# First block's boundaries reordered and the second softmax of the differential heads left in PSUM

## The chip, the cores and the metric

The kernel runs on one core of one Trainium2 chip. A core has a matrix engine (PE, TensorE) and three engines for element work: DVE (VectorE), ACT (ScalarE) and POOL (GpSimd). Each works through its own instructions in program order and waits on semaphores for the others. SP issues the DMA transfers of the weights. Matrix products land in PSUM, eight banks of 128 partitions x 512 fp32; everything else is in SBUF. The metric is the device time of one execution in microseconds; the kernel before takes 1145.21 us (median of 3 runs, 1144.27 to 1145.81).

## The reference

Two transformer stacks run one behind the other on one sequence of 256 tokens, width 1024, fp32. The first is one block with three sublayers: feed-forward, a mixer of two attentions, feed-forward.

```python
mods = (silu(c) @ w_ada + b_ada).reshape(B, 9, 1024)   # shift, scale, gate of 3 sublayers
n = modulate(rmsnorm(h, g_pre[0]), shift(0), scale(0))
h = h + 0.5 * gate(0) * rmsnorm(swiglu(n, ...), g_post[0])
n = modulate(rmsnorm(h, g_pre[1]), shift(1), scale(1))
p = n @ w_in            # qa, ka, va, qi, ki, wi, qb, kb, vb
# oa: each query keeps the top 64 keys of an index score sum_h relu(qi_h . ki) * wi_h, then softmax
# ob: stick-breaking attention
h = h + gate(1) * rmsnorm(concat(oa, ob) @ w_out, g_post[1])
n = modulate(rmsnorm(h, g_pre[2]), shift(2), scale(2))
h = h + 0.5 * gate(2) * rmsnorm(swiglu(n, ...), g_post[2])
```

The second has two layers. The first of them begins with differential attention, 8 heads of two softmaxes each; the other has latent attention, and both have a squared-ReLU network.

```python
q, k, v = split(rms_norm(h, g) @ w_qkv)       # q, k rotated; (B, S, 8 heads, 2, 64), v (B, S, 8, 128)
p = softmax(where(causal, q @ k.T * 64 ** -0.5, -inf))
a = p[:, :, 0] - lam * p[:, :, 1]             # the two softmaxes of a head, combined
o = rms_norm(a @ v, subln_g, 1e-5) * (1 - lambda_init)
h = h + o @ w_o
```

## The kernel before

**Precision and tiles.** A product is three passes: each weight tile of 128 x 1024 is split into `wh` (ACT, L475) and `wl`, raw minus `wh` (DVE or POOL by `st["lo"]`, L481), and each activation likewise into `nh` and `nl`; the PE multiplies `wh` by `nh`, `wh` by `nl` and `wl` by `nh` (`mm`, L534). So nothing can be multiplied until both halves of its activation are there.

**Weights.** They come in one fixed order in pieces of up to 512 KB over SP's queue into a ring of seven `raw` tiles. `pump` takes the next piece from the ring and issues its split, as far ahead of the PE as `st["ahead"]` lets it. Pieces of the modulation matrix (`ada`) are mixed in: for one of them ACT first writes eight copies into an accumulator (L445), and DVE adds the piece to it (L448). As the engines work in order, a piece that is pumped stands in front of everything that is issued after it on ACT and on DVE or POOL.

**PSUM.** Four banks belong to accumulators (`abank`); the other four (`bank`, tile name `mm`) are a ring for transposes, scores and small products.

**Entry into a sublayer of the first block.** `enter_block1` ends one sublayer and begins the next for two row blocks of 128 tokens. `tail` is the rest of the old product; `Post` normalizes and adds it (`sq`: square sum, L594; `u_`: product with the gain, L658; `b`: inverse root; `c`: the sum into h, L669). `Pre1` normalizes h for the new sublayer (`stat`, `r_`, `yy`: L688), transposes it in eight tiles of 128 (`T`, L619), modulates each tile by its column's scale and shift (`mod`, DVE L642 or ACT L640), and splits the result into `nh` (ACT, L709) and `nl` (DVE, L712). p0 and q0 stand for row block 0, p1 and q1 for row block 1. `direct` modulates on ACT straight into `nh`, while DVE modulates the same tiles again into a PSUM bank (`y2_`), from which the low half is formed. `mid[0]` and `mid[1]` are the first products of the new sublayer that are put between. The function runs twice: into the mixers (the first entry, up to about 235 us), where `mid` is `kiva`, the product for the index keys, the index weights and part of the values, and into the second feed-forward network (the second entry, 365 to 395 us), where `mid` is `f2.mul` of `Ffn2` and `f2.act` is silu (L927) and its product with the other half (L928).

**Index keys.** `keys()` (L1223) normalizes the index keys, copies the values, and has the keys transposed (L1240) and written back by ACT (L1241, `kiT`). The scores, their sum over heads (DVE, L1263) and the search for the top 64 (DVE, `topk`) follow; in that search POOL makes the low halves of the weights.

**Differential heads.** For each pair of heads `qk_finish` rotates queries and keys (DVE L1476, L1478, POOL L1480) and transposes them. `head` multiplies them into two banks, one for each softmax, and `softmax_bank` takes each to its exponentials: DVE adds the mask and finds the extremum (L1487) into the SBUF tile `s`, and ACT takes the exponential in place (L1490). Then DVE combines the two (L1572, `SCALAR_TENSOR_TENSOR`, two pieces of 256 and 128 columns), the PE transposes the result (L619) and multiplies it with v.

## Time and profile before

| | |
|---|---|
| median of 3 runs | 1145.21 us (1144.27 to 1145.81) |
| the profiled execution | 1145.55 us, of it the span 1143.7 us |
| PE busy | 1102.1 us (96% of the span) |
| DVE busy | 745.5 us (65%) |
| ACT busy | 610.0 us (53%) |
| POOL busy | 147.2 us (13%) |
| mean granted clock of the PE | 0.991 |

The span is the time from the first to the last instruction that the profiler recorded. A share of busy time is a mean over stages: an engine busy for 65% of the span can be full for 30 us in one of them. The granted clock is a share of the PE's full 2.4 GHz; 0.5 is its lower level, 1.2 GHz. A row of the timeline has a start, a duration (several like instructions in one row have a common duration) and, in brackets, the idle time before it with the instruction that ended it. `nl<-mm,nh` means that tile `nl` is written from `mm` and `nh`; buffer numbers are left out.

### The profile page before, as it was taken

To read this page: it belongs to the slowest core of one execution; us is meant where nothing else is said; L and a number is where in the kernel's file an instruction comes from. 1 tells how busy PE (TensorE), PEld (TensorE's weight loads), DVE (VectorE), ACT (ScalarE), POOL (GpSimd) and SP (SyncE) were. 2 spreads that over 40 slices of the span, in tenths; PEclk is the share of its full clock that TensorE was granted. 3 is DMA by queue.
4 is the path that set the end of the run, shared out by engine and by line. 5 is a ranking of instruction groups with operands and counts; after the bars stand their busy time and mean duration, and the time that the engine had idled before them with its cause. 6 is when DMAs were issued, how large, how long until landed. Compare 5 with 4: busy or idle time off the path is not lost. (4 is left out here: it accounts for less than half of the span.)

```text
span 1143.7 us, 18702 instructions
## 1 busy us (share of the span) xinstructions
PE 1102.1 (96%) x7156; PEld 994.6 (87%) x7156; DVE 745.5 (65%) x1306; ACT 610.0 (53%) x1181; POOL 147.2 (13%) x203
## 2 busy tenths in 40 slices
PE   6999999999999899999999899999999999999997
PEld 5998999888887799999877779999999888999996
DVE  6978777789686865554655457555566766655554
ACT  5564445654676643443564666444457665544442
POOL 1002000214002000000069840000002200000001
PEclk8999999999999999999999999999999999999999
DMA  9979897377565485555444245555544533655541
GB/s 324 403 244 352 332 335 229 121 251 294 168 208 198 166 313 189 180 186 185 164 148 147 99 161 175 193 185 186 189 159 138 194 111 138 248 187 188 191 136 38
DMA packets 65915, 230.26 MB, mean 201 GB/s; under 512 B 7272, under 2 KB 8688, under 8 KB 65696
## 3 DMA queue, kind: packets, MB, share of 16 engines
q1 hardware_dynamic: 63792, 225.06, 56.4%
q10 hardware_dynamic: 1776, 3.29, 0.8%
q8 instruction: 56, 0.92, 0.3%
q0 software_dynamic: 256, 0.71, 0.3%
q14 instruction: 35, 0.29, 0.1%
HBM read 227.97 MB, written 2.63 MB: 202 GB/s over the span
## 5 line engine op out<-in xcount | busy, mean ns | idle before, releaser
L481 DVE TENSOR_TENSOR wl<-raw,wh 128x1024 fp32r<-128x1024 f32 (+3 forms) x319 | 381.6, 1212 | 75.1 <-ACT wh L475 74.9
L475 ACT ACTIVATE wh<-raw 128x1024 fp32r<-128x1024 f32 (+3 forms) x350 | 355.3, 1035 | 29.2 <-DMA raw<-in_stream_dram 26.1
L534 PE MATMUL mm<-nl,wh 128*128 128x256 f32 x1128 | 314.3, 283 | 0.0
L534 PE MATMUL mm<-nh,wh 128*128 128x256 f32 x1128 | 314.1, 283 | 0.0
L534 PE MATMUL mm<-nh,wl 128*128 128x256 f32 x1128 | 314.1, 283 | 0.0
L534 PEld LDWEIGHTS mm<-nh,wh 128*128 128x128 f32 x1128 | 214.2, 192 | 3.1
L534 PEld LDWEIGHTS mm<-nl,wh 128*128 128x128 f32 x1128 | 214.2, 192 | 3.0
L534 PEld LDWEIGHTS mm<-nh,wl 128*128 128x128 f32 x1128 | 213.8, 192 | 0.1
L534 PE MATMUL acc<-wh,fh 128*128 128x512 f32 x372 | 120.8, 392 | 0.0
L534 PE MATMUL acc<-wh,fl 128*128 128x512 f32 x372 | 119.8, 389 | 0.3 <-DVE fl L904 0.3
L534 PE MATMUL acc<-wl,fh 128*128 128x512 f32 x372 | 119.8, 389 | 0.0
L481 POOL TENSOR_TENSOR wl<-raw,wh 128x256 fp32r<-128x256 f32 (+2 forms) x124 | 91.0, 773 | 197.8 <-ACT wh L475 197.8
L1086 ACT ACTIVATE rl<-mm 128x256 f32<-128x256 f32 x64 | 24.6, 384 | 159.0 <-PE mm L534 159.0
L591 POOL TENSOR_TENSOR sm<-sm,nhalf 128x1 f32<-128x1 f32 (+1 forms) x36 | 22.4, 624 | 629.1 <-DVE sm L600 561.2
L1087 DVE TENSOR_TENSOR ff<-rl 128x256 f32<-128x256 f32 x64 | 27.2, 425 | 101.8 <-ACT rl L1086 101.8
L899 ACT ACTIVATE sg<-mm 128x256 f32<-128x256 f32 x38 | 14.5, 382 | 139.2 <-PE mm L534 139.2
L534 PEld LDWEIGHTS acc<-wh,fl 128*128 128x128 f32 x372 | 69.9, 188 | 15.7 <-DVE fl L904 0.9
L534 PEld LDWEIGHTS acc<-wl,fh 128*128 128x128 f32 x372 | 69.9, 188 | 15.0
L534 PE MATMUL acc<-wh,nh 128*128 128x512 f32 (+3 forms) x216 | 80.4, 395 | 0.5 <-ACT nh L709 0.4
L534 PE MATMUL acc<-wh,nl 128*128 128x512 f32 (+3 forms) x216 | 77.2, 380 | 3.6 <-DVE nl L712 3.6
L534 PE MATMUL acc<-wl,nh 128*128 128x512 f32 (+3 forms) x216 | 76.6, 377 | 0.0
L534 PEld LDWEIGHTS acc<-wh,fh 128*128 128x128 f32 x372 | 65.5, 189 | 9.1
(316 smaller groups left out, 1591.8 us busy)
## 6 DMA issues: line engine op xcount, KB each, us to landing
raw<-in_stream_dram SPq DMA_DIRECT2D x395, 512.0 KB, 4.6
raw<-in_stream_dram SPq DMA_DIRECT2D x16, 448.0 KB, 8.9
raw<-in_stream_dram SPq DMA_DIRECT2D x8, 384.0 KB, 3.7
raw<-in_stream_dram SPq DMA_DIRECT2D x8, 292.0 KB, 2.9
gp<-in_rows_dram SPq DMA_DIRECT2D x3, 512.0 KB, 6.6
wide<-scr ACTq DMA_DIRECT2D x1, 1536.0 KB, 9.9
raw<-in_stream_dram SPq DMA_DIRECT2D x4, 320.0 KB, 2.7
h<-in_x_dram SPq DMA_DIRECT2D x4, 256.0 KB, 3.5
```

What stands on the lines that cost most here:

```text
L475: act.activation(wh[:, 0:n], raw, AF.Copy)
L481: e.tensor_tensor(wl[:, u:v], raw[:, u:v], wh[:, u:v].bitcast(F32), op=ALU.subtract)
L534: pe.matmul(o, l, r, start=start, stop=True, skip_group_check=True)
L591: pool.tensor_tensor(o, v, nhalf[:, 0:v.shape[-1]], op=ALU.pow)
L899: act.activation(sg, ps[:, 0:S], AF.Silu)
L1086: act.activation(rl, ps[:, 0:S], AF.Relu)
L1087: dve.tensor_tensor(ff, rl, rl, op=ALU.mult)
```

## The change

There are four edits.

1. **POOL's pieces.** Where POOL makes a low half of more than 512 columns, it does so in two pieces and not in four.
2. **The boundary code.** `direct` is gone: every modulated tile is written once, and both halves are formed from it. In row block 0 the first four tiles are modulated by DVE into two PSUM banks, two tiles in each; the last four are modulated by ACT into SBUF. In row block 1 DVE's four and ACT's four all go into SBUF. High and low halves are formed in pairs of tiles. `p1.u_(0)` stands behind the first low halves of row block 0. `mid[0]` is issued ahead of the pumped weights, and a new argument, `aside`, is issued ahead of the transposes of row block 1; the second entry gives it `f2.act(0)`, which stood behind the whole entry.
3. **The index keys.** The constant `G5` (8) is written out; its loops keep their order. The last of eight `pump` calls in the loop over k moves behind `begin(keys())`.
4. **The heads.** `softmax_bank` can write its exponentials to another place than it reads. For the second softmax of each head that place is the PSUM bank which held its scores, and the combine reads it there.

```diff
@@ -50,7 +50,6 @@
 EL1 = ((1, 2), 1)
 EL2 = ((0, 1), 0)
 G4 = 7
-G5A = 8
 GSP = {2: 1, 8: 1}
 LO0 = "pool"
 YH = (1, 1, 1, 1, 1)
@@ -475,10 +474,10 @@
         act.activation(wh[:, 0:n], raw, AF.Copy)
         c = n * {"dve": 8, "alt": 4, "pool": 0}.get(st["lo"], st["lo"]) // 8
         for e, a, b in ((dve, 0, c), (pool, c, n)):
-            step = b - a if e is dve or b <= a else (b - a) // (4 if b - a > 512 else 2)
-            for u in range(a, b, step or 1):
-                v = min(u + step, b)
-                e.tensor_tensor(wl[:, u:v], raw[:, u:v], wh[:, u:v].bitcast(F32), op=ALU.subtract)
+            m = (a + b + 1) // 2 if b - a > 512 and e is pool else b
+            for u, v in ((a, m), (m, b)) if b > a else ():
+                if v > u:
+                    e.tensor_tensor(wl[:, u:v], raw[:, u:v], wh[:, u:v].bitcast(F32), op=ALU.subtract)
         st["w"] += 1
         tiles[key] = (wh, wl)
 
@@ -672,7 +671,7 @@
     class Pre1:
         def __init__(self, i, n, t):
             self.i, self.n, self.t, self.ss = i, n, t, small(2)
-            self.y, self.tp = [None, None], [None, None]
+            self.y, self.tp, self.y2 = [None, None], [None, None], {}
 
         def stat(self, hf):
             square_sum(half(self.t, hf), D, self.ss[:, hf:hf + 1])
@@ -691,28 +690,21 @@
             self.tp[hf] = transposes(self.y[hf], 4)
 
 
-        def y2_(self, a, b, on_act=False):
-            if a == 0:
-                self.y2 = [bank() for _ in range(2)]
+        def y2_(self, a, b, on_act=False, psum=False):
+            y = (bank() if psum else w512("y2"))[:, 0:(b - a) * P].rearrange("p (a b) -> p a b", b=P)
             for k in range(a, b):
-                c = slice(k % 4 * P, k % 4 * P + P)
-                mod(self.i, k, self.y2[k // 4][:, c], self.tp[k // 4][:, c], on_act)
-
-        def direct(self, a, b):
-            for k in range(a, b):
-                mod(self.i, k, self.n[0][:, k, tk(self.t)], self.tp[k // 4][:, k % 4 * P:k % 4 * P + P], True)
-
-        def y2v(self, a, b):
-            return self.y2[a // 4].rearrange("p (a b) -> p a b", a=4)[:, a % 4:a % 4 + b - a, :]
-
-        def hi(self, a, b):
-            act.activation(self.n[0][:, a:b, tk(self.t)], self.y2v(a, b), AF.Copy)
-
-        def lo(self, a, b):
-            dve.tensor_tensor(self.n[1][:, a:b, tk(self.t)], self.y2v(a, b),
-                              self.n[0][:, a:b, tk(self.t)].bitcast(F32), op=ALU.subtract)
-
-    def enter_block1(tail, acc, G, i, n, mid, table, early, late):
+                mod(self.i, k, y[:, k - a, :], self.tp[k // 4][:, k % 4 * P:k % 4 * P + P], on_act)
+                if k % 2 == 0:
+                    self.y2[k] = y[:, k - a:k - a + 2, :]
+
+        def hi(self, k):
+            act.activation(self.n[0][:, k:k + 2, tk(self.t)], self.y2[k], AF.Copy)
+
+        def lo(self, k):
+            dve.tensor_tensor(self.n[1][:, k:k + 2, tk(self.t)], self.y2[k],
+                              self.n[0][:, k:k + 2, tk(self.t)].bitcast(F32), op=ALU.subtract)
+
+    def enter_block1(tail, acc, G, i, n, mid, table, early, late, aside=None):
 
         p0, p1 = Post(acc, G, 0), Post(acc, G, 1)
         q0, q1 = Pre1(i, n, 0), Pre1(i, n, 1)
@@ -737,38 +729,49 @@
             pump_n(k)
         tail.go(1, 0, m)
         p1.sq(0)
-        p1.u_(0)
         q0.T(0)
         q0.T(1)
         tail.go(1, 1, m)
-        q0.direct(0, 2)
-        q0.y2_(0, 4)
-        q0.lo(0, 2)
-        q0.hi(2, 4)
-        q0.lo(2, 4)
+        q0.y2_(0, 2, psum=True)
+        q0.hi(0)
+        q0.y2_(2, 4, psum=True)
+        q0.lo(0)
+        q0.hi(2)
+        q0.lo(2)
         p1.sq(1)
+        p1.u_(0)
         p1.b()
         p1.u_(1)
         q0.y2_(4, 8, True)
-        q0.hi(4, 8)
+        q0.hi(4)
+        q0.hi(6)
         p1.c(0)
         q1.stat(0)
         p1.c(1)
-        q0.lo(4, 8)
+        q0.lo(4)
         q1.stat(1)
+        q0.lo(6)
         q1.r_()
+        mid[0]()
         st["lo"] = "dve"
         pump_n(late)
         q1.yy(0, False)
         q1.yy(1, False)
-        mid[0]()
+        if aside:
+            aside()
         q1.T(0)
         q1.T(1)
-        for k in range(0, 8, 2):
-            q1.direct(k, k + 2)
-            q1.y2_(k, k + 2)
-            q1.lo(k, k + 2)
+        q1.y2_(0, 2)
+        q1.hi(0)
+        q1.y2_(2, 4)
+        q1.lo(0)
+        q1.hi(2)
+        q1.lo(2)
+        q1.y2_(4, 8, True)
         mid[1]()
+        for k in (4, 6):
+            q1.hi(k)
+            q1.lo(k)
 
     def enter_block2(tail, add, pres, first, stats=None, early=0, each=(0, 0, 0)):
 
@@ -1200,22 +1203,18 @@
                 A[t], B[t] = abank(), abank()
             mode_b([A[t][:, 0:292], B[t][:, 0:292]], nh[:, k, tk(t)], nl[:, k, tk(t)], w, 0, 292, k == 0)
 
-        G5 = G5A
-
         def mid(a, b):
             for k in range(a, b):
                 kiva(k, 0)
 
-        enter_block1(tail, acc0, G[0], 1, n, (lambda: mid(0, G4), lambda: mid(G4, G5)),
+        enter_block1(tail, acc0, G[0], 1, n, (lambda: mid(0, G4), lambda: mid(G4, 8)),
                      lambda: act.preload_act_table_set("natural_log_exp_and_others"), *EL1)
         st["lo"] = "dve"
-        for k in range(G5):
+        for k in range(8):
             kiva(k, 1)
-            st["rel"] += 1
-            pump(3)
-        for k in range(G5, 8):
-            kiva(k, 0)
-            kiva(k, 1)
+            if k < 7:
+                st["rel"] += 1
+                pump(3)
         st["ahead"] = 3
         va = w1k("va").rearrange("p (a b) -> p a b", a=2)
         flags = {}
@@ -1241,7 +1240,7 @@
             act.activation(kiT, tp[:, 0:S], AF.Copy, scale=cl[:, C_KIDX:C_KIDX + 1])
 
         begin(keys())
-        st["rel"] += 8 - G5
+        st["rel"] += 1
         pump()
         qiT = w1k("qiT").rearrange("p (a b) -> p a b", a=4)
         z = [w256("z0"), w256("z1")]
@@ -1479,7 +1478,7 @@
                               op=ALU.mult)
         ROPE_E.tensor_tensor(o.rearrange("p (a b) -> p a b", b=64), t1, t2, op=ALU.add)
 
-    def softmax_bank(s, ps, su):
+    def softmax_bank(s, ps, su, o=None):
 
 
         mn = small(2)
@@ -1487,7 +1486,8 @@
             dve.tensor_tensor_reduce(out=s[:, c0:c0 + W], in0=ps[:, c0:c0 + W], in1=cmaskw[:, c0:c0 + W], scale=1.0,
                                      scalar=3.0e38, op0=ALU.add, op1=ALU.min, accum_out=mn[:, t:t + 1])
         for t, c0, W in BLK:
-            act.activation(s[:, c0:c0 + W], s[:, c0:c0 + W], AF.Exp, bias=mn[:, t:t + 1], scale=-1.0, accum_out=su[t])
+            act.activation((s if o is None else o)[:, c0:c0 + W], s[:, c0:c0 + W], AF.Exp, bias=mn[:, t:t + 1],
+                           scale=-1.0, accum_out=su[t])
 
 
     nlam = cp.tile([P, 1], F32, name="nlam")
@@ -1559,8 +1559,8 @@
             half_rows(pss, lambda pr, t, W: (QK[pr, c, tk(t)], QK[pr, 2 + c, 0:W]), True)
             for j in range(2):
                 s = w512("s")
-                softmax_bank(s, pss[j], [su[:, 2 * j + t:2 * j + t + 1] for t in range(2)])
-                e.append(s)
+                softmax_bank(s, pss[j], [su[:, 2 * j + t:2 * j + t + 1] for t in range(2)], pss[j] if j else None)
+                e.append(pss[j] if j else s)
             for _ in range(YH[0]):
                 yield
             inv, cf = small(4), small(2)
@@ -1873,8 +1873,7 @@
     n = new_n()
     f2 = Ffn2(n)
     enter_block1(tail, acc1, G[1], 2, n, (lambda: f2.mul(0, (0, 1, 2, 3)), lambda: None),
-                 lambda: act.preload_act_table(AF.Silu), *EL2)
-    f2.act(0)
+                 lambda: act.preload_act_table(AF.Silu), *EL2, lambda: f2.act(0))
     f2.mul(1, (0, 1))
     f2.out(0)
     f2.mul(1, (2, 3))
```

The changed order can be read from the instructions of each engine. First DVE at the second entry, before; `u` is the product of `Post`, `mm` a bank, `h_89` row block 1 of h:

```order
L658 TENSOR_TENSOR u<-acc,G 128x512
L642 TENSOR_SCALAR mm<-mm,ac_a,ac_b 128x128 x4
L712 TENSOR_TENSOR nl<-mm,nh 128x2x128 x2
L600 TENSOR_SCALAR sm<-sm 128x1
L658 TENSOR_TENSOR u<-acc,G 128x512
L669 SCALAR_TENSOR_TENSOR h_89<-u,sm,h_89 128x512 x2
L712 TENSOR_TENSOR nl<-mm,nh 128x4x128
L600 TENSOR_SCALAR sm<-sm 128x1
L688 TENSOR_SCALAR y<-h_89,sm 128x512 x2
L642 TENSOR_SCALAR mm<-mm,ac_a,ac_b 128x128 x2
```

And the same place now, where `y_4191` and `y_4252` are SBUF tiles of modulated values:

```order
L641 TENSOR_SCALAR mm<-mm,ac_a,ac_b 128x128 x4
L704 TENSOR_TENSOR nl<-mm,nh 128x2x128 x2
L657 TENSOR_TENSOR u<-acc,G 128x512
L599 TENSOR_SCALAR sm<-sm 128x1
L657 TENSOR_TENSOR u<-acc,G 128x512
L668 SCALAR_TENSOR_TENSOR h_89<-u,sm,h_89 128x512 x2
L704 TENSOR_TENSOR nl<-y_4191,nh 128x2x128 x2
L599 TENSOR_SCALAR sm<-sm 128x1
L687 TENSOR_SCALAR y<-h_89,sm 128x512 x2
L931 TENSOR_TENSOR sg<-sg,acc 128x256
L641 TENSOR_SCALAR y_4252<-mm,ac_a,ac_b 128x128 x2
L641 TENSOR_SCALAR y_4256<-mm,ac_a,ac_b 128x128 x2
```

The modulations of row block 0 and their low halves stand ahead of the first u; the low half of its last four tiles is formed from an SBUF tile in two pairs, and the silu product (L931) stands ahead of row block 1's modulations.

Next ACT at the end of the first entry, before; `wh` and `ada` belong to pumped pieces, `junk` to the keys' square sums, `va` to the values, `kiT` to the transposed keys:

```order
L640 ACTIVATE nh<-mm,ac_b,ac_a 128x128 x8
L475 ACTIVATE wh<-raw 128x1024 x3
L445 ACTIVATE ada<-kc,cl 128x128 x8
L594 ACTIVATE junk,sm<-acc 128x64 x2
L1230 ACTIVATE va<-acc 128x220 x2
L1236 ACTIVATE va<-acc 128x292 x2
L1300 ACTIVATE qiT<-mm 128x256
L1241 ACTIVATE kiT<-mm,cl 128x256
```

And now:

```order
L639 ACTIVATE y_2481<-mm,ac_b,ac_a 128x128 x4
L701 ACTIVATE nh<-y_2481 128x2x128 x2
L474 ACTIVATE wh<-raw 128x1024 x2
L593 ACTIVATE junk,sm<-acc 128x64 x2
L1229 ACTIVATE va<-acc 128x220 x2
L1235 ACTIVATE va<-acc 128x292 x2
L474 ACTIVATE wh<-raw 128x1024
L444 ACTIVATE ada<-kc,cl 128x128 x8
L1299 ACTIVATE qiT<-mm 128x256
L1240 ACTIVATE kiT<-mm,cl 128x256
```

The square sums and the values now stand ahead of the third weight copy and of the eight copies for `ada`, which come directly before the transposed queries and keys.

Last ACT in the heads, the exponentials of one head before:

```order
L475 ACTIVATE wh<-raw 128x1024
L1490 ACTIVATE s,sm<-s,sm 128x256
L1490 ACTIVATE s,sm<-s,sm 128x128
L1490 ACTIVATE s,sm<-s,sm 128x256
L1490 ACTIVATE s,sm<-s,sm 128x128
L475 ACTIVATE wh<-raw 128x1024
```

And now:

```order
L474 ACTIVATE wh<-raw 128x1024
L1489 ACTIVATE s,sm<-s,sm 128x256
L1489 ACTIVATE s,sm<-s,sm 128x128
L1489 ACTIVATE mm,sm<-s,sm 128x256
L1489 ACTIVATE mm,sm<-s,sm 128x128
L474 ACTIVATE wh<-raw 128x1024
```

The second pair of exponentials is written to a bank.

## Rows read from the trace of the kernel before

**Rows 1.** First part of the page: busy time, share of the span, instructions.

```profile
PE 1102.1 (96%) x7156; PEld 994.6 (87%) x7156; DVE 745.5 (65%) x1306; ACT 610.0 (53%) x1181; POOL 147.2 (13%) x203
...
```

**Rows 2.** Waits of the PE engine: waiting line <- releaser: total us, times, longest.

```profile
...
PE mm L619 <- DVE s L1572: 4.7, 4, 2.9
...
PE acc L534 <- DVE nl L712: 3.6, 4, 1.1
...
PE mm L619 <- DVE sg L928: 2.1, 1, 2.1
...
```

**Rows 3.** Timeline of the second entry: start, duration (us), engine, line, work, [idle before <-releaser].

```profile
...
366.75 0.69 DVE L658 TENSOR_TENSOR u<-acc,G 128x512 f32<-128x512 f32 x1 [1.26 <-ACT junk L594]
...
367.45 1.78 DVE L642 TENSOR_SCALAR mm<-mm,ac_a,ac_b 128x128 f32<-128x128 f32 x4
...
369.74 0.50 PE L534 MATMUL acc<-wh,nl 128*128 128x512 f32 x1 [1.11 <-DVE nl L712]
...
376.22 1.04 PE L619 MATMUL mm<-kc,y 128*128 128x128 f32 x8
...
381.60 0.81 ACT L640 ACTIVATE nh<-mm,ac_b,ac_a 128x128 fp32r<-128x128 f32 x2 [1.48 <-DVE mm L642]
...
382.56 2.01 ACT L475 ACTIVATE wh<-raw 128x1024 fp32r<-128x1024 f32 x2
...
384.16 0.44 PE L619 MATMUL mm<-kc,sg 128*128 128x128 f32 x2 [2.13 <-DVE sg L928]
...
388.78 0.28 PE L534 MATMUL mm<-nh,wh 128*128 128x256 f32 x1
...
392.01 0.41 DVE L928 TENSOR_TENSOR sg<-sg,acc 128x256 f32<-128x256 f32 x1
...
394.53 0.38 PE L619 MATMUL mm<-kc,sg 128*128 128x128 f32 x2
...
```

**Rows 4.** Windows: stretch, length, busy PE PEld DVE ACT POOL, granted clock, DMA share, GB/s.

```profile
251.00:279.00 28.00, 27.67 (x219) 25.92 (x217) 27.93 (x77) 9.57 (x16) 15.16 (x16) 1.00 0.79 287
385.00:389.00 4.00, 4.00 (x13) 3.13 (x12) 3.44 (x4) 4.00 (x11) 0.00 (x0) 0.57 0.56 182
631.00:635.00 4.00, 3.95 (x19) 3.51 (x20) 0.62 (x1) 2.92 (x9) 4.00 (x7) 0.58 0.09 26
...
```

**Rows 5.** Timeline of the heads, POOL, DVE and PE.

```profile
...
607.91 2.83 POOL L481 TENSOR_TENSOR wl<-raw,wh 128x256 fp32r<-128x256 f32 x4
...
609.02 0.68 DVE L1476 TENSOR_TENSOR ropes<-acc,ropa 128x512 f32<-128x512 f32 x1
...
620.66 4.25 DVE L1572 SCALAR_TENSOR_TENSOR s<-s,sm 128x256 f32<-128x256 f32 x2
...
624.70 0.59 PE L619 MATMUL mm<-kc,s 128*128 128x128 f32 x3 [0.35 <-DVE s L1572]
...
626.10 0.67 DVE L1476 TENSOR_TENSOR ropes<-acc,ropa 128x512 f32<-128x512 f32 x1
...
630.40 1.22 DVE L1572 SCALAR_TENSOR_TENSOR s<-s,sm 128x256 f32<-128x256 f32 x2
...
630.94 1.21 PE L619 MATMUL mm<-kc,s 128*128 128x128 f32 x3 [2.89 <-DVE s L1572]
...
650.58 0.44 PE L619 MATMUL mm<-kc,s 128*128 128x128 f32 x2 [1.20 <-DVE s L1572]
...
```

**Rows 6.** Groups of POOL by form: count | busy us, mean ns | idle before.

```profile
...
L481 POOL TENSOR_TENSOR wl<-raw,wh 128x256 fp32r<-128x256 f32 x108 | 80.8, 788 | 32.9 <-ACT wh L475 32.9
...
L1480 POOL TENSOR_TENSOR ro<-ropes 128x512 f32<-128x512 f32 x8 | 10.2, 1290 | 2.3 <-DVE ropes L1478 1.9 <-PE acc L534 0.5
...
```

**Rows 7.** Timeline of the first entry's end, ACT, PE and DVE.

```profile
...
227.36 2.44 ACT L445 ACTIVATE ada<-kc,cl 128x128 f32<-128x128 f32 x8
...
232.38 0.33 PE L1240 MATMUL mm<-kc,kt 128*128 128x128 f32 x1 [1.90 <-DVE kt L1233]
...
238.03 1.41 DVE L1263 SCALAR_TENSOR_TENSOR z<-rl,wi,z 128x256 f32<-128x256 f32 x4 [0.38 <-ACT rl L1259]
...
```

## The prediction

> **What bounds the kernel now.** I read the first part of the page first. The PE is busy for 1102.1 of 1143.7 us, 96%, and no other engine passes 65% [rows 1]. Only three things can therefore move the time by more than noise: a stretch where the PE waits, a stretch where its clock falls, and a new wait. The waits of the PE engine come next. The longest line is 4.7 us on L619 behind the combine of the differential heads (L1572). Two others belong to the boundary code of the first block: 3.6 us for the low halves (L712) and 2.1 us for the silu product before the second feed-forward network (L928) [rows 2]. I then read the timeline around each place, forward and backward from its waiting row. In the second use of `enter_block1` ("second entry" here; the one at the mixers is the first) the PE stands at 369.74 and at 384.16 [rows 3]. In the heads it stands at 624.70, 630.94 and 650.58 [rows 5]. At the end of the first entry it stands at 232.38 [rows 7]. Last come the windows. The granted clock is below full after two of these waits: 0.57 over 385 to 389 and 0.58 over 631 to 635 [rows 4]. It is a mixture of the levels 2.4 and 1.2 GHz. Each stretch loses 4 x 0.43 or 4 x 0.42, that is 1.7 us of PE work. Both fell behind waits of over 2 us (2.13 and 2.89); the wait of 1.90 at 232.38 was not followed by a fall in what I read.
>
> **The change part by part.** The sum is made against the profiled execution, 1145.55 us (span 1143.7, and 1.85 around it). The median of the runs shown, 1145.21, is 0.34 lower, so 0.34 goes off at the end.
>
> *Second entry.* Before, DVE forms u (0.69) ahead of the four modulations (1.78), and the first low half follows them; the PE gets it at 369.74 after 1.11 of waiting [rows 3]. After, u stands behind the low halves, so the modulations start some 0.7 sooner, and the first low half waits for two of them instead of four (0.9 less). The wait shrinks to about 0.3. Of the 3.6 us of low-half waits, about 2.6 lie in this entry [rows 2] (the rest, about 1.0, in the first). The transposes of row block 1 come at 375.5 instead of 376.22, since what precedes them on DVE and ACT moves up by that 0.7. The silu product moves ahead of them, so that the wait of 2.13 at 384.16 goes, and with it, I take it, the 1.7 of half clock. For the PE alone: 2.6 + 2.13 + 1.7 = 6.4 less the new wait for row block 1. That block's first pair of modulations costs 2 x 0.445 and its split about 0.46, then the low half 0.45, all behind the transposes: 1.8. So the PE alone would be 4.6 ahead.
>
> It does not keep all of it. ACT works in order and leads to the next product. Its first split of row block 1 can begin 0.9 behind the end of the transposes (376.22 + 1.04 - 0.7 = 376.6), at 377.5. Two splits of 0.4, four modulations of 0.4 (half of the 0.81 row at 381.60, which also shows ACT waiting 1.48 for DVE before; that alternation goes) and two splits more make 3.2, with 0.3 for handovers 381.0. That is 1.5 before the two weight copies of 382.56 [rows 3]. From these copies to the second silu product (392.01) before takes 9.45, ACT and DVE passing weight tiles and modulation sums between them; nothing in that piece is changed. So this product comes at 390.5, ends at 390.9, and its transposes follow at about 391.2, where they stood at 394.53. The gain here is **3.3**, with the PE waiting at that spot for the rest. Bounds: 1.5, when the transposes move only as ACT does, and 4.6, when the PE keeps everything.
>
> *Heads.* Before, both inputs of the combine are in SBUF. Seven of the eight pairs look like that at 630.40 (1.22, POOL starting 0.3 behind). The pair at 620.66 took 4.25, all while POOL made low halves in pieces of 0.79 [rows 5, 6]. A pair of like shape on an idle POOL has 1.41 / 2 = 0.70 (the row of four at 238.03) [rows 7]. After, one input lies in PSUM. The trace has no such combine, so I bound it: at best 0.70; at worst it still loses to POOL, 4.25. The nearest row decides: the rope product at 609.02 reads one PSUM and one SBUF operand while POOL works on low halves (607.91 to 610.74), and takes 0.68; with no low half running the same form has 0.67 at 626.10 [rows 5]. I take 0.70. In row terms: the wait of 0.35 at 624.70 goes. The rope, minimum and exponentials of the next head, queued on DVE behind the slow combine, come 3.55 sooner; of the 2.89 at 630.94 about 0.3 is left, 2.6 gained. The half-clock stretch behind it goes with it, 1.7. At 650.58 two combines in a row are shortened by 0.5 each, and of the 1.20 and what follows it 0.8 goes. Sum **5.4**; from 2.6 (half of that wait and 1.2 elsewhere) to 7.0 if PE idle at every head shrinks as well. The second softmax's bank is held until the combine has read it, where it was free after the minimum. This adds a possible wait at one point only, the scores of the last head, which take the ring's slot of the head before; by that point the combine is over 1.4 us earlier than the PE gets there, so I count nothing. If that cover were missing, the PE would stand there for up to 1.4.
>
> The Trainium skill, "SBUF — State Buffer", section "Who interferes with whom", says that a DVE instruction with at most one SBUF input leaves GpSimd alone, and that with two it shares a read interface on which the second to issue is fully blocked until the first ends. By that the new combine is free, as the 0.68 row has it. The blocked pair of 620.66 does not follow it: it waited about 3.6 more than 0.70, over four pieces of 0.79, not the rest of one.
>
> *POOL's pieces.* 27 low-half tiles go from four pieces to two. One piece of 512 should cost about 1.29, as the sum of equal shape does in L1480, so a tile takes 2.6 instead of 3.15, or less [rows 6]. POOL is busy for 13% of the span [rows 1], and I count nothing for its shorter time. The cost may be elsewhere: a two-input DVE instruction that has to wait for a piece waits up to 1.29, not 0.79.
>
> *First entry.* The keys' square sums and the rescaled keys now come before the last tile's copies, so the eight ACT copies of 2.44 no longer stand in front of them, and the wait of 1.90 at 232.38 and a shorter one behind it go: 2.6 [rows 7]. But the same 2.44, with a weight copy of about 1.0, now stands in front of the evacuation of the keys' transposes, and the PE waits there for some 1.4. With the 1.0 of low-half waits it would stand about 2.2 ahead at the scores. Then DVE is the bound: 27.93 of 28 us busy from 251 to 279 [rows 4], and the first softmax waits for it. Only what DVE's own score sums gain counts, about 1.2. Against it stand five two-input instructions of that stretch beside POOL's pieces. Each may lose 0.5 more (1.29 less 0.79); half of them do: 1.2. I take **0**, between a loss of 2.5 (all five lose 0.5) and a gain of 2.5 (all that the PE has).
>
> Sum: 3.3 + 5.4 + 0 = 8.7. 1145.55 - 8.7 - 0.34 = 1136.5 us.
>
> **The rivals.** *DVE's full stretch takes it back.* POOL's longer pieces block all five instructions (2.5), the PE, which arrives earlier, idles for more than 2 us at the first softmax, and its clock falls (1.7): 1136.5 + 4.2 = 1140.7. For it speaks DVE's 27.93 of 28; against it that DVE's chain starts earlier. The same page of the Trainium skill speaks for it, since by its section on the shared port the second to issue waits for the whole piece; the row of 4.25 bears it out in kind.
>
> *The heads stay as they are.* The combine waits for something other than POOL, or the rope chain is late anyway: only 3.3 is gained, 1145.21 - 3.3 = 1141.9. The 0.68 row speaks against it.
>
> *Everything is kept by the PE.* The second entry gives 4.6 and the first 2.5: 1145.21 - 4.6 - 5.4 - 2.5 = 1132.7. Against it stands ACT's order.
>
> *Slower.* The combine still loses to POOL, and as each piece is now up to 1.29 long, it loses in more than one head. Each starved head costs 0.35 + 2.6 + 1.7 = 4.65, and the entries' 3.3 decides: from one head more on the kernel is slower (1145.21 - 3.3 + 4.65 = 1146.6); three more give 1155.9. For it speaks that in the seven other heads DVE issued only 0.3 before POOL; against it the 0.68 row with POOL busy.
>
> **How the numbers follow.** Forecast 0.55, DVE's stretch 0.13, heads unchanged 0.14, all kept 0.10, slower 0.08. A measurement of this kernel can tell about 0.2% (2.3 us) from no change, so "faster" is below 1142.9. Forecast, DVE's stretch and all kept count as faster but for a tail of 0.04; of the unchanged heads 0.08 do; the rest of these and 0.01 of the slower case are "same". That gives 0.82, 0.11 and 0.07. With every bound at its end the forecast's own sum reaches from 1145.21 - 4.6 - 7.0 - 2.5 = 1131.1 to 1145.21 - 1.5 - 2.6 + 2.5 = 1143.6. The upper end needs three mishaps at once, so I stop the range of 1131 to 1142.5 short of it; it takes in the first three rivals and leaves out about 0.2: the slower case, 0.08 of the unchanged heads at worse ends, and tails.
>
> **What would show it.** In the profile after: the combine pairs all at about 0.7, none over 1.3 (the heads' step); no wait over 1 us on L619 behind it, and a clock of 1.00 from 631 on; u behind the low halves and the wait at 369.74 below 0.5 (second entry); no wait behind the silu product at 384, a clock of 1.00 there, and the second transposes about 3 earlier relative to the start of that entry, with a PE wait just before them (ACT's chain). In the first entry the waits on the keys' product gone, one of about 1.4 on its evacuation, and a longer stand at the first softmax. I am wrong if a combine of over 2 us is still there, or if the stand at the first softmax takes more than 2 us with a clock below 1.00 behind it.

## The result and the profile after

The changed kernel takes 1125.63 us (median of 4 runs, 1124.44 to 1129.59), against 1145.51 (4 runs, 1144.27 to 1147.11): a ratio of 0.9832, 95% interval 0.9803 to 0.9860. A second set on another occasion gave 0.9851 (0.9822 to 0.9880). The forecast was 1136.5, with a range of 1131 to 1142.5. So the direction was right and the gain about twice what was predicted. Of 64 later runs of the kernel before, one of 6122 us was in another state and is left out of every comparison below.

First the page of the kernel after, the row that answers to [rows 1], busy time by engine:

```profile
PE 1097.0 (98%) x7156; PEld 992.1 (88%) x7156; DVE 733.4 (65%) x1300; ACT 608.7 (54%) x1181; POOL 135.9 (12%) x141
...
```

The waits of its PE engine, for [rows 2]:

```profile
...
PE acc L533 <- DVE nl L704: 0.8, 2, 0.6
PE mm L618 <- DVE sg L931: 0.6, 1, 0.6
...
PE mm L533 <- ACT kiT L1240: 0.6, 1, 0.6
...
PE mm L618 <- DVE s L1572: 0.3, 1, 0.3
...
```

The combine went from 4.7 to 0.3 and the low halves from 3.6 to 0.8. The wait of 2.1 at the first silu product is gone; the 0.6 on that line now stands in front of the second one, where the forecast put a wait. The wait on the keys' product is gone, and one of 0.6 on its evacuation (`kiT`) has come. The high half of row block 1 has a wait of 1.15 at the second entry (367.79), where 1.8 was forecast for that block.

The order of the PE is the same in both programs, instruction by instruction, so the two profiles can be laid over one another by the PE's instruction number. That shows where the 20.9 us between the profiled executions (1145.55 and 1124.63) lie:

| stretch | the PE's lead there | |
|---|---|---|
| start, up to 27 us | 3.9 us | unchanged code |
| first entry, up to the scores | 3.9 to 8.4 | later still 8.9 |
| second entry | 8.9 to 14.3 | 5.4 |
| heads | 14.3 to 20.2 | 5.9 |
| the rest of the PE's work, to its last instruction | 20.2 to 19.9 | -0.3 |

About 0.9 more lies behind the last PE instruction; x2, x3 and x6 below, whose code there is that of before, have it too: it comes and goes with unchanged code. The forecast had 0, 0, 3.3 and 5.4 for the first four.

The second entry after, in the timeline, for [rows 3]; the whole program stands 8.9 earlier here, so 8.9 is added to compare:

```profile
...
357.49 1.65 DVE L641 TENSOR_SCALAR mm<-mm,ac_a,ac_b 128x128 f32<-128x128 f32 x4 [0.36 <-PE mm L618]
...
358.40 0.39 ACT L701 ACTIVATE nh<-mm 128x256 fp32r<-128x256 f32 x1 [0.60 <-DVE mm L641]
...
359.93 0.68 DVE L657 TENSOR_TENSOR u<-acc,G 128x512 f32<-128x512 f32 x1
...
365.61 1.03 PE L618 MATMUL mm<-kc,y 128*128 128x128 f32 x8
...
366.56 1.36 DVE L641 TENSOR_SCALAR y<-mm,ac_a,ac_b 128x128 f32<-128x128 f32 x4
...
367.32 0.42 ACT L701 ACTIVATE nh<-y 128x256 fp32r<-128x256 f32 x1 [1.13 <-DVE y L641]
367.96 0.42 ACT L701 ACTIVATE nh<-y 128x256 fp32r<-128x256 f32 x1 [0.22 <-DVE y L641]
...
370.27 2.01 ACT L474 ACTIVATE wh<-raw 128x1024 fp32r<-128x1024 f32 x2
...
370.71 0.38 PE L618 MATMUL mm<-kc,sg 128*128 128x128 f32 x2
...
```

u stands behind the modulations. The transposes of row block 1 come at 374.5, 1.7 sooner than before, where 0.7 was forecast. ACT's two weight copies come at 379.2 instead of 382.56: 3.4 sooner, where 1.5 was forecast. The second silu transposes, 394.53 before, follow at 380.18 + 8.9 = 389.1.

The three ACT rows that write `nh` show where ACT waits for DVE now, in row block 0 (358.40, and 0.39 more behind it) and in row block 1. Before, two rows of these places read:

```profile
...
369.72 0.39 ACT L709 ACTIVATE nh<-mm 128x256 fp32r<-128x256 f32 x1 [2.31 <-DVE nl L712]
...
378.61 1.50 ACT L640 ACTIVATE nh<-mm,ac_b,ac_a 128x128 fp32r<-128x128 f32 x4 [0.94 <-DVE mm L642]
...
```

With the 1.48 of 381.60 [rows 3] that made 4.7 us of ACT waiting for DVE; now it is 0.60 + 0.39 + 1.13 + 0.22 = 2.3.

The end of the first entry after, in the timeline, for [rows 7]:

```profile
...
224.32 0.38 PE L1239 MATMUL mm<-kc,kt 128*128 128x128 f32 x2
...
225.00 2.45 ACT L444 ACTIVATE ada<-kc,cl 128x128 f32<-128x128 f32 x8
...
228.13 0.92 PE L533 MATMUL mm<-kiT,qiT 64*128 64x256 f32 x8 [0.56 <-ACT kiT L1240]
...
231.39 1.40 DVE L1262 SCALAR_TENSOR_TENSOR z<-rl,wi,z 128x256 f32<-128x256 f32 x4
...
```

The eight copies of ACT do stand in front of `kiT` now, as foreseen; the PE waits 0.56 for it, not 1.4. DVE's first score sum comes at 231.39, 6.6 sooner than at 238.03, of which 3.9 are the start's and 2.8 the entry's own. The PE's stand at the first softmax is 1.08, as before (1.10), where a longer one was foreseen: DVE's work moved forward as far as the PE did.

The windows after, for [rows 4]: the top-64 search, the stretch behind the silu product, and the heads; the third number from the end is the granted clock.

```profile
242.00:270.00 28.00, 27.99 (x224) 26.45 (x222) 27.93 (x80) 10.02 (x16) 13.49 (x8) 1.00 0.91 320
371.00:375.00 4.00, 4.00 (x24) 3.49 (x24) 2.71 (x3) 4.00 (x11) 0.00 (x0) 1.00 0.29 88
610.00:640.00 30.00, 28.34 (x151) 22.07 (x149) 14.24 (x60) 22.20 (x64) 24.01 (x23) 1.00 0.41 129
...
```

DVE is as full as before in the search (27.93 of 28), and the clock is at its full level in all three.

The combine after, from the groups by form (mean ns of one), for [rows 5]:

```profile
...
L1572 DVE SCALAR_TENSOR_TENSOR s<-mm,sm,s 128x256 f32<-128x256 f32 x8 | 3.9, 484 | 0.3
...
L1572 DVE SCALAR_TENSOR_TENSOR s<-mm,sm,s 128x128 f32<-128x128 f32 x8 | 2.7, 342 | 0.0
...
```

All eight pairs take the same time, none waits. As rows of the timeline the pairs last 0.74, where 0.70 was forecast. POOL's pieces, for [rows 6]:

```profile
...
L480 POOL TENSOR_TENSOR wl<-raw,wh 128x512 fp32r<-128x512 f32 x54 | 71.8, 1359 | 36.1 <-ACT wh L474 36.1
...
```

54 pieces of 1.36, where 1.29 was forecast; 71.8 us in all instead of 80.8.

### The profile page after: what moved, and what is told of

It is laid out like the page before. It is cut to its first block, busy times and chain, and to the rows that moved or that the text cites. A ratio compares the mean times of both kernels' runs of the same rounds, so it can differ in the third digit from the quotient of the medians.

```text
span 1122.9 us, 18616 instructions
## 1 busy us (share of the span) xinstructions
PE 1097.0 (98%) x7156; PEld 992.1 (88%) x7156; DVE 733.4 (65%) x1300; ACT 608.7 (54%) x1181; POOL 135.9 (12%) x141
## 4 chain that ended last, share of the span: by engine, by line
PE 82%; DVE 6%; ACT 6%; issue 3%; POOL 3%; DMA 1%; SPq 0%; POOLq 0%; DVEq 0%; ACTq 0%
PE acc L533 41%; PE mm L533 38%; DVE wl L480 2%; ACT wh L474 1%; POOL wl L480 1%; PE mm L618 1%; ACT s L1344 1%; ACT ada L444 1%; ACT s L1489 1%; DVE raw L438 1%; POOL sm L590 1%; DMA h<-in_x_dram 1%; ACT junk L593 0%; DMA raw<-in_stream_dram 0%; POOL ro L1479 0%
## 5 line engine op out<-in xcount | busy, mean ns | idle before, releaser
L480 POOL TENSOR_TENSOR wl<-raw,wh 128x512 fp32r<-128x512 f32 (+2 forms) x62 | 79.8, 1315 | 202.6 <-ACT wh L474 202.6
```

The lines of the kernel that those rows point to most:

```text
L480: e.tensor_tensor(wl[:, u:v], raw[:, u:v], wh[:, u:v].bitcast(F32), op=ALU.subtract)
```

## The experiments

Each edit of the change was made alone on the kernel before (labels x), or undone alone in the changed kernel (labels a). Times in profiles are compared from a common PE instruction, so that what happened earlier in the program drops out. The columns of this table are worked out so: at the first entry from PE instruction 1201 (182.46 in before), at the second from a matmul shortly before it (358.28 in before). The end of the search is the start of DVE's first instruction that reads its result (`sel`, 271.43 in before).

| kernel | first score sum | end of the search | ACT's weight copies, 2nd entry | second silu transposes |
|---|---|---|---|---|
| before | 55.6 | 89.0 | 24.3 | 36.2 |
| changed | 52.8 | 83.9 | 20.9 | 30.8 |
| boundary code alone (x3) | 52.0 | 85.4 | 20.9 | 30.8 |
| silu ahead alone (x5) | 55.6 | 89.0 | 24.0 | 33.9 |
| row block 1 alone (x6) | 53.8 | 87.2 | 22.5 | 32.5 |
| row block 0 alone (x7) | 55.1 | 88.5 | 22.6 | 33.0 |
| keys alone (x4) | 55.3 | 87.4 | 24.3 | 34.6 |
| changed, u first | 53.3 | 84.4 | 21.5 | 31.4 |
| changed, keys as before | 52.3 | 84.9 | 20.9 | 30.8 |
| changed, quarters | 52.5 | 84.6 | 20.9 | 30.8 |

**x1: POOL's halves alone.**

```diff
-            step = b - a if e is dve or b <= a else (b - a) // (4 if b - a > 512 else 2)
-            for u in range(a, b, step or 1):
...
+            m = (a + b + 1) // 2 if b - a > 512 and e is pool else b
+            for u, v in ((a, m), (m, b)) if b > a else ():
```

> Before with POOL's low halves in two pieces alone. By the prediction (a longer piece can only block longer): 0 to 2.5 us slower, the five two-input DVE instructions beside POOL's pieces in the top-64 search at 1.5 us or more. Rival (fewer pieces meet DVE less often, as the profile after has them all at 1.23 to 1.28): 1 to 2 us faster there, the combine of the heads' first pair still over 1.2. If the 3.6 us at the start of the program come from this edit, another 3.6 faster; if they are chance, the start reads like one or the other profile without regard to the edit.

Measured: 0.9995 (0.9981 to 1.0009), no difference that can be told. In the profile the long two-input instructions in the search take 1.28, 1.89, 1.27, 1.28, 1.27 and 1.22, where before had 1.28, 1.49, 1.51, 1.50, 1.49 and 1.75: from the last score sum to the end of the search 19.8 instead of 20.6, so 0.8 is gained there. But the combine, still with two SBUF inputs, reads like this in the groups by form:

```profile
...
L1572 DVE SCALAR_TENSOR_TENSOR s<-s,sm 128x128 f32<-128x128 f32 x8 | 11.0, 1372 | 0.0
...
L1572 DVE SCALAR_TENSOR_TENSOR s<-s,sm 128x256 f32<-128x256 f32 x8 | 3.9, 485 | 0.3
...
```

The second instruction of each pair now waits for one longer piece (1372 ns; in before 817 to 833 in seven pairs), as the forecast feared for two-input instructions. No pair starves over several pieces in this profile; but POOL's run of pieces ended 0.15 ahead of the third pair here, so it doesn't show that halves would not starve it. Both signs occurred, in different places. (The first score sum comes 1.4 later than in before in this profile, behind a fall of the clock at 230.)

**x2: the heads alone.**

```diff
-                softmax_bank(s, pss[j], [su[:, 2 * j + t:2 * j + t + 1] for t in range(2)])
-                e.append(s)
+                softmax_bank(s, pss[j], [su[:, 2 * j + t:2 * j + t + 1] for t in range(2)], pss[j] if j else None)
+                e.append(pss[j] if j else s)
```

> Before with the second softmax of a head left in its bank, nothing else. By the prediction the combine needs only one SBUF operand and takes 0.7 a pair beside POOL's quarter pieces too: 5.4 (the profile after shows 6.0 between the second entry and the end of the heads), so 1139.5 to 1140. Rival (the longer pieces are what ended the stall): a combine of over 2 us is still there and under 3 us are gained.

Measured: 0.9967 (0.9951 to 0.9982), 3.8 us. By the PE's instructions 5.1 are gained in the heads. The groups by form:

```profile
...
L1573 DVE SCALAR_TENSOR_TENSOR s<-mm,sm,s 128x256 f32<-128x256 f32 x8 | 3.9, 484 | 0.3
...
L1573 DVE SCALAR_TENSOR_TENSOR s<-mm,sm,s 128x128 f32<-128x128 f32 x8 | 2.7, 342 | 0.0
...
```

They are those of the changed kernel to the nanosecond, beside POOL's quarters. In the timeline, the pair that starved in before (620.66) runs in the middle of 13 pieces that follow one another on POOL:

```profile
...
615.42 9.09 POOL L481 TENSOR_TENSOR wl<-raw,wh 128x256 fp32r<-128x256 f32 x13
...
620.97 0.74 DVE L1573 SCALAR_TENSOR_TENSOR s<-mm,sm,s 128x256 f32<-128x256 f32 x2
...
```

So the operand's place ends the stall, not the size of the pieces. This is what the Trainium skill states ("SBUF — State Buffer", "Who interferes with whom"): one SBUF input, no contention.

**x3: the boundary code alone.** The edit is part 2 of the change with its last line:

```diff
-        q0.direct(0, 2)
-        q0.y2_(0, 4)
...
+        q0.y2_(0, 2, psum=True)
+        q0.hi(0)
...
-    f2.act(0)
+                 lambda: act.preload_act_table(AF.Silu), *EL2, lambda: f2.act(0))
```

> Before with the new order inside enter_block1 alone (silu ahead of the transposes included), at both entries; keys, pieces and heads as before. By the prediction 3.3 at the second entry and nothing kept at the first. By the profile after 5.6 at the second entry; at the first the 2.2 of its low and high halves, kept if DVE isn't full there, lost by the end of the top-64 search if it is: 5.6 to 7.8 faster.

Measured: 0.9912 (0.9894 to 0.9931), 10.1 us, more than both expectations. The table shows where: at the first entry DVE's first score sum comes 3.6 sooner and all of it is kept to the end of the search (89.0 to 85.4); at the second the columns equal those of the changed kernel. By the PE's instructions that is 9.0 up to the end of the second entry.

**x4: the keys alone.**

```diff
-        for k in range(G5):
+        for k in range(8):
             kiva(k, 1)
-            st["rel"] += 1
-            pump(3)
+            if k < 7:
+                st["rel"] += 1
+                pump(3)
...
-        st["rel"] += 8 - G5
+        st["rel"] += 1
```

> Before with the index keys started ahead of the last pumped tile, nothing else. By the prediction the 2.6 of waits on the keys' product go, about 1.4 come back on its evacuation, and DVE's full stretch leaves nothing at the first softmax: 0. By the profile after (PE 2.6 ahead at the scores and still so at the end of the search): 2 to 3 us faster, with no or little growth of the stand before the first softmax.

Measured: 0.9994 (0.9982 to 1.0006), nothing that can be told. That is the 0 of the prediction, but not by its reason. The PE gets 2.9 ahead at the keys' product, gives back 0.8 at its evacuation, and stands longer at the first softmax, as the timeline says (1.10 at the same place before, 279.96):

```profile
...
278.20 0.72 PE L619 MATMUL mm<-kc,s 128*128 128x128 f32 x3 [2.02 <-ACT s L1343]
...
383.76 0.44 PE L619 MATMUL mm<-kc,sg 128*128 128x128 f32 x2 [2.12 <-DVE sg L928]
...
```

And its windows, of the stretches behind these two waits and of one between them:

```profile
279.60:283.00 3.40, 3.40 (x18) 2.62 (x18) 2.61 (x4) 2.04 (x5) 0.00 (x0) 0.51 0.41 129
324.00:327.40 3.40, 3.40 (x9) 2.69 (x9) 1.11 (x2) 3.27 (x7) 0.00 (x0) 0.50 0.21 70
384.00:388.00 4.00, 4.00 (x25) 3.50 (x24) 3.43 (x4) 4.00 (x11) 0.00 (x0) 1.00 0.43 150
...
```

The rival "DVE's full stretch takes it back" has these two signs, a stand of over 2 us at the first softmax and a fall of the clock behind it. But DVE took back only part: the search ends 1.6 sooner (87.4 against 89.0), and the first softmax starts 1.6 sooner. The fall behind it costs the PE 1.5, but at 300.5 it is 1.6 ahead again, at a place where it waits for ACT's `pT` (0.88 in before, 0.47 here). What takes the lead to 0.25 is the fall at 324, behind a wait of 1.5 (on ACT's `aTs`, L1400) that every profile has. The clock did not fall behind the silu product, although the wait there was 2.12 (2.13 in before, where the clock went to 0.57 in [rows 4]). A wait of this length is followed by a fall in some executions and not in others.

**The changed kernel once more.**

> The changed kernel once more, nothing edited, for the comparison with before on one chip and a second profile. If the 3.6 us at the start of the program belong to the change, this profile has the early weight copies as the first one had them, without the 2.5 us wait of before; if they vary from run to run, the times here scatter by some 5 us, as those of before do (1140.2 to 1148.9), and the middle lies some 17 to 18 us under before instead of 20.

Measured: 0.9851 (0.9822 to 0.9880); 5 runs, 1125.89 to 1129.70. The waits of its PE in the first 27 us:

```profile
...
24.67 0.74 PE L533 MATMUL acc<-nh,wh 128*128 128x256 f32 x4 [2.09 <-ACT wh L474]
...
```

The same stand was 2.54 in before and is missing in the first profile after. Laid over that one by PE instructions, this profile is 3.6 later from here on, with nothing edited; x1 and x6, whose code at the start is that of before, have the early start (3.7 and 3.5 ahead of before), and others lie between. So the early start of the first profile varies from run to run and is no part of the change. Over all runs the changed kernel has a median of 1126.7 (9 runs), the kernel before 1144.5 (63 runs, 1139.4 to 1149.8): 17.8.

**The changed kernel with the keys as before.**

```diff
-            if k < 7:
-                st["rel"] += 1
-                pump(3)
+            st["rel"] += 1
+            pump(3)
...
-        st["rel"] += 1
```

> The changed kernel with the index keys started behind the last pumped tile, as before. By the wait it gives back (3.2 less 0.6 at the keys' product) it is 2.6 slower than the changed kernel. Rival, after the keys alone gave 0.7 of 1144: the first softmax's end is set by DVE, whose first score sum comes no sooner with the keys ahead; then 0 to 1 slower.

Measured: 0.9857 (0.9830 to 0.9884), 1127.53 beside 1127.91 for the changed kernel on that chip: the rival. The first score sum comes even 0.5 sooner without the early keys, and the search ends 1.0 later (84.9 against 83.9); 0.6 of that is one sum for `ada` that took 1.91 instead of 1.28 beside POOL. So this part of the change is worth 1 us by the profile; the runs can't tell it from nothing.

**The changed kernel with quarters.** The edit of x1 the other way round.

> The changed kernel with POOL's low halves in four pieces, as before. By the prediction 0 to 2.5 faster (a shorter piece blocks DVE for less). By the profiles since, where the five long two-input instructions in the top-64 search took 1.49 to 1.75 beside quarters and 1.28 beside halves: 0.8 to 1.4 slower, all of it before the first softmax; the heads the same, as their combine no longer needs two SBUF operands.

Measured: 0.9864 (0.9836 to 0.9892), 1128.89 beside 1127.91, as the second forecast has it. The search ends 0.7 later (84.6), and its sums for `ada` look again as before:

```profile
...
249.80 1.52 DVE L447 SCALAR_TENSOR_TENSOR ada<-raw,sc,ada 128x1024 f32<-128x1024 f32 x1
...
```

**x5: silu ahead alone.**

```diff
         mid[0]()
+        if aside:
+            aside()
         q1.T(0)
```

> Before with the silu of row block 0 (second entry) ahead of row block 1's transposes, nothing else. If silu alone carries the second entry: the wait of 2.13 goes and the weight copies on ACT come 0.4 sooner, 3 to 4 us with the clock. If it only lets the PE arrive at the second silu product sooner and ACT's and DVE's chain to that product sets the time: 0.5 to 1, a wait of 1 to 2 us in front of the second transposes.

Measured: 0.9987 (0.9970 to 1.0004), nothing that the runs can tell. In the profile the wait at the first silu product goes and the clock doesn't fall there, which puts the PE 3.9 ahead; then it stands for the second product, and 2.3 is left:

```profile
...
391.48 0.44 PE L619 MATMUL mm<-kc,sg 128*128 128x128 f32 x2 [1.44 <-DVE sg L930]
...
```

So the mechanism of the forecast is right: ACT's and DVE's chain to the second silu product sets the time, and a lead of the PE alone is lost there. Of the 2.3, 1.6 are the clock, since without a fall before's own order gives 34.6 (x4).

**x6: row block 1 alone.**

```diff
-            q1.direct(k, k + 2)
-            q1.y2_(k, k + 2)
-            q1.lo(k, k + 2)
...
+        q1.z_(0, 2)
+        q1.zhi(0)
...
+        q1.z_(4, 8, True)
```

(`z_`, `zhi` and `zlo` are the `y2_`, `hi` and `lo` of the change under other names.)

> Before with the new way through row block 1 alone, at both entries: four tiles modulated by DVE into SBUF, four by ACT, halves in pairs; row block 0, silu, keys and pieces as before. By the prediction (ACT's way through this block 0.2 to 0.5 shorter): nothing at the first entry, at the second the weight copies on ACT under 0.7 sooner. Rival (tile by tile, ACT and DVE waited for each other on one bank, which I did not count): ACT leaves the block 1.5 to 2 us sooner at both entries, the first score sum on DVE and the second silu product come as much sooner; 1.5 to 4 us in all.

Measured: 0.9941 (0.9919 to 0.9963), 6.8 us (the early start is in this profile, not necessarily in the runs). The rival, and more in the runs than its 4: ACT's weight copies come 1.7 sooner at the second entry, the first score sum 1.7 sooner at the first, and the PE keeps 4.1 in all by the profile. The PE's stand for the keys goes from 1.90 to 0.76 with it, the one for the silu product from 2.13 to 0.36, and on average the clock took 1.9 less in these runs than in those of before. In the timeline the transposes of row block 1 and the copies are 4.6 apart, in before 6.3 [rows 3]:

```profile
...
372.35 1.04 PE L619 MATMUL mm<-kc,y 128*128 128x128 f32 x8
...
376.97 2.02 ACT L475 ACTIVATE wh<-raw 128x1024 fp32r<-128x1024 f32 x2
...
```

**x7: row block 0 alone.**

```diff
-        p1.u_(0)
         q0.T(0)
...
-        q0.direct(0, 2)
-        q0.y2_(0, 4)
+        q0.z_(0, 2, psum=True)
+        q0.zhi(0)
...
+        p1.u_(0)
         p1.b()
```

> Before with the new way through row block 0 alone, at both entries (two banks, u behind the first low halves, halves in pairs); row block 1, silu, keys and pieces as before. By the prediction row block 1's transposes come 0.7 sooner. By the profile after they come 1.8 sooner at the second entry, since the inverse root of row block 1 stood behind this block's halves on ACT and DVE; the wait for the low half at 369.74 is below 0.3. With the silu still behind the entry: 1.5 to 2.5 us in all.

Measured: 0.9978 (0.9961 to 0.9996), 2.5 us. The transposes of row block 1 come 1.7 sooner at the second entry, and ACT's copies too (22.6). With the 1.7 of x6 that makes the 3.4 of the whole boundary code, so that nothing is left for the earlier place of `mid[0]`, which was not tried alone. At the first entry the clock fell at 230 in this profile, behind the PE's stand for the keys, so its score sum shows only 0.5. The wait for the silu product is unchanged, and no fall is behind it:

```profile
...
381.27 0.44 PE L619 MATMUL mm<-kc,sg 128*128 128x128 f32 x2 [2.12 <-DVE sg L945]
...
```

**The changed kernel with u first.**

```diff
+        p1.u_(0)
         q0.T(0)
...
-        p1.u_(0)
         p1.b()
```

> The changed kernel with the first u of row block 1 ahead of row block 0's modulations, as it stood before. By the prediction u is what delays them: the first low half 0.7 later at each entry, 1 to 1.5 us slower. Rival (DVE is idle ahead of them, until the transposes are there): no difference.

Measured: 0.9850 (0.9822 to 0.9878), 1127.27: no difference that the time can show. In the profile it costs 0.6 at the second entry (21.5 against 20.9) and 0.5 at the first, 1.1 in all, as the first forecast has it. So u is worth what its 0.69 says, and the transposes' other 1.1 come from the rest of row block 0's new way.

**The changed kernel with whole pieces on POOL.**

```diff
-            m = (a + b + 1) // 2 if b - a > 512 and e is pool else b
+            m = b
```

> The changed kernel with POOL's low halves in one piece of 1024. If each end of a piece is where DVE's two-input work gets caught, one fewer: the five long instructions of the top-64 search at 1.28 or one of them over 2, 0 to 1 us faster. If a longer piece makes the rope sums and the PE wait for POOL in the heads: 1 to 3 slower, with new waits on POOL there.

Measured: 0.9921 (0.9895 to 0.9946), 1136.14 beside 1127.91 for the changed kernel: some 8 us of the gain are lost, more than either forecast has. DVE's sum is caught behind a piece in the search (timeline):

```profile
...
250.11 1.28 DVE L447 SCALAR_TENSOR_TENSOR ada<-raw,sc,ada 128x1024 f32<-128x1024 f32 x1
250.94 5.08 POOL L480 TENSOR_TENSOR wl<-raw,wh 128x1024 fp32r<-128x1024 f32 x2 [22.94 <-ACT wh L474]
...
253.65 3.45 DVE L447 SCALAR_TENSOR_TENSOR ada<-raw,sc,ada 128x1024 f32<-128x1024 f32 x1
...
```

Two of these take 3.45 and 3.43 instead of 1.28, and the search ends at 89.6 instead of 83.9. That is the price which the prediction set against the halves, and it exists; at 512 columns it happened not to be paid in the changed kernel. The 2.17 more fit inside one piece of about 2.5. This agrees with the Trainium skill ("SBUF — State Buffer", "Who interferes with whom"), by which the shared port is held for a whole instruction and the other engine is blocked until it ends. By the profile 5.6 of the 8 are lost up to the first softmax. Another 1.1 is a stand of the PE for POOL's rope sums (1.20 at 581.32), which the second forecast had.

## Why the prediction was wrong

The gain is 17 to 19 us in the runs and was forecast as 8.7. Point by point:

**The heads: right.** 5.4 forecast, 5.9 in the profile of the change, 5.1 and 3.8 alone by profile and by runs. The pairs at 0.74, the 0.3 left of the wait and the operand's place as the cause all came as stated. Of the 5.4, the three waits made 3.75 and the clock 1.7. Over the runs of x2 the clock took no less than in before on the same chip (10.8 on average against 9.7), so their 3.8 fits the waits alone.

**The second entry: right in its mechanism, one term mis-sized.** It was said that the PE's lead doesn't last and that ACT's way to the second silu product decides; x5 shows just this. From the weight copies to the second silu product the changed kernel takes 9.44, as before (9.45). The term that failed is "1.5 before the two weight copies": 3.4 was measured. Two parts of it were short. Row block 1's transposes came 1.7 sooner, not 0.7. I had counted u alone (0.6 by the kernel with u first); the other 1.1 is the rest of row block 0's new way, which x7 has alone: there ACT's wait of 2.31 for DVE (369.72) became two of 0.60 and 0.39. And from the transposes to the copies took 4.66 instead of 6.34, where my walk left 5.5: ACT began 0.7 and not 0.9 behind their end, and its eight instructions took 2.95 where I had 3.5. What went is waiting. Tile by tile, ACT wrote `nh` and DVE modulated the same pair of tiles, each waiting for the other: ACT for 1.48 at 381.60, which the prediction names, and for 0.94 at 378.61, which it doesn't. x6, which changes this block alone, gets the whole 1.7.

A smaller reading was wrong too: of the low halves' 3.6, 2.1 lie in this entry and 1.5 in the first, not 2.6 and 1.0; the 3.3 doesn't use it. And 1.6 of the 5.4 in the profiles is luck: before's profile has a fall of the clock behind the silu product, and without it before's own order gives 34.6 instead of 36.2 (x4).

**The first entry: wrong.** "I take 0" was 5.0. The step that failed is that only 1.2 of the lead reaches DVE's score sums. The search was indeed the bound and DVE just as full. But DVE's chain starts where ACT's way through row block 1 ends, and so it gained what the weight copies of the second entry gained: 3.6 for the boundary code alone (x3), all kept. In the first entry of before ACT waited for DVE in the same way:

```profile
...
223.81 0.81 ACT L640 ACTIVATE nh<-mm,ac_b,ac_a 128x128 fp32r<-128x128 f32 x2 [1.49 <-DVE mm L642]
...
```

The same way of ACT was in both entries, and its gain was counted in one sum and not in the other. On top come the halves, 0.7 (a gain, where I charged 1.2), and the keys with some 1 or less. Alone, the keys gave 1.6 up to the first softmax in the profile, where I had nothing; the runs show no gain (x4).

**The clock: mis-sized by certainty.** I put two falls, 3.4, into the sum as if they belonged to the waits of over 2 us. Among five profiles with the unchanged silu wait of 2.1 (before, x1, x2, x4, x7) the fall behind it appears in two; among six with the heads' wait of 2.9 (before, x3 to x7) in four. So each should have been a fraction of 1.7. And the stand of 1.90 for the keys, which I left without a fall, has one behind it in three of five profiles (x1, x2, x7, not before and x5). Other places, the first softmax and a point near 320, showed falls in some profiles, those of the changed kernel and its variants too. Over all runs the time that the granted clock took (span times one less its mean) was 9.8 us for before (63 runs) and 4.5 for the changed kernel (9 runs). So up to 5 of the 17 us come through the clock; a fall can cost less than it takes, as behind the first softmax in x4. I had 3.4, from other reasons.

**The start: chance.** 3.9 of the profiled difference at the start, and the 0.9 behind the last PE instruction, come and go with unchanged code.

**The rivals.** Slower and the unchanged heads are excluded by x2. "DVE's full stretch takes it back" did not happen: the search ended sooner in the changed kernel and with the keys alone. "All kept by the PE" (1132.7) was nearest, and it too was short: it had 4.6 and 2.5 for the entries, and 5.4 and 5.0 were measured. Alone, boundary code, heads, keys and halves sum to 10.1 + 3.8 + 0.7 + 0.6 = 15.2, beside 17.1 to 19.2 for the whole by the two ratios. How much of the 2 to 4 between them is interaction and how much the scatter of such runs stays open.

## What to carry to other kernels

Where two engines alternate on a tile, read the length of the old stretch as work plus waiting before you price the new one; brackets like 0.94 and 1.48 on its rows are the sign. A term that feeds two sums (here ACT's way through a row block) should be bounded once and carried into both. And a stretch of lower clock behind a wait counts with the share of profiles that show it, not with its full length.

## What the runs showed of the hardware

- What a two-input DVE instruction loses beside POOL is no steady function of the piece's length. In the same search five of the long ones took 1.49 to 1.75 beside pieces of 256 columns (before), all 1.28 beside 512 (but one 1.9 in x1 and with the keys as before), and two took 3.45 beside 1024. So where the pieces fall against them matters beside their length.
- In x1, where the combine had two SBUF inputs, each pair waited once for one piece of 512. Beside pieces of 256 one pair in eight waited for over four, 3.96 to 3.98 us in all six profiles of that kind (before, x3 to x7). The first agrees with the Trainium skill ("SBUF — State Buffer", "Who interferes with whom"), by which the blocked instruction waits until the other one ends; the second goes beyond that.
- Between the start and the end of the program the clock fell in stretches of 3.4 us, once 6.8 in the heads of x7, and these moved from run to run between a few places.
- DVE's modulation of a 128 x 128 tile took 0.34 from PSUM into SBUF (1.36 for four) and 0.41 from PSUM into PSUM (1.65 for four) in the same kernel.
